# One encoder layer on one core: later weight splits, other fillers and seven ramp pairs instead of eight in the first pass over h

## The chip, the cores and the metric

The kernel runs on one core of a Trainium2 chip. The metric is the device time of one execution in microseconds (us). The engines are TensorE (PE, products and transpositions), VectorE (DVE), ScalarE (ACT), GpSimd (POOL) and SyncE (SP, which here issues most transfers). Each engine executes its instructions in the order in which they are written for it, and waits for semaphores of the others.

## The reference

One layer for x of 1024 rows and 2048 columns, all in fp32:

```python
mod = jax.nn.silu(c) @ w_ada + b_ada
shift, scale, gate = jnp.split(mod, 3, axis=-1)
h = rmsnorm(x, pre_g) * (1.0 + scale[:, None]) + shift[:, None]
proj = h @ w_in
q, k, v, gate_a, u, gate_p = jnp.split(proj, SPLIT_POINTS, axis=-1)
y_a = windowed_gqa(q, k, v, rel_table, sink) * jax.nn.silu(gate_a)
y_p = multiscale_pool(u, w_pool_grp, pool_scale) * jax.nn.silu(gate_p)
g = jax.nn.sigmoid(h @ w_merge + b_merge)
g_a, g_p = jnp.split(g, N_BRANCHES, axis=-1)
merged = g_a * (y_a @ w_br_attn) + g_p * (y_p @ w_br_pool)
o = merged @ w_out
return x + gate[:, None] * rmsnorm(o, post_g)
```

The change lies in the first third of `h @ [w_in, w_merge]`: in how h is made, and how the first columns of weights meet it.

## The kernel before, in words

**Products.** Each fp32 operand is split into a high part (ACT copies it to a format of fewer bits) and a low part (DVE subtracts); a product is then three matmuls, hi·hi, hi·lo and lo·hi. Around this stands one level of Strassen's scheme: h is held transposed in quarters, for each part j of k (four parts per pass, each of two 128-row tiles) as seven operands B11, T3, T2, B21, T4, T1, B22, each as h and l (high and low). `strassen` takes a pair of weight columns (256) and makes seven products over its parts j, into banks called X, V and Z; the sums of these (p, u) are DVE's. One pair over four parts j is 7 × 3 × 4 = 84 matmuls of 128x512, over two parts 42.

**The first pass** goes over the first half of k for 34 pairs in the order ORDER. Since h's parts become ready one by one, it has stages:

1. The start. x comes in rows (`fetch_rows_of_x`, 16 transfers for each half s of the rows). `norm_rows` squares (two pieces on ACT, two on DVE), sums (DVE) and takes the root (ACT, L428); `scale_rows` scales on DVE; PE transposes 128x128 blocks (XT); `take_turned` copies them to xT.
2. adaLN's columns. w_ada comes in groups j of 256 columns. `modulation` multiplies them by silu(c) in four steps (GEMV on PE, four k tiles in each), copies the sums (acc, ACT), transposes them (PM) and puts them into modc (DVE). In the start, `warm(n)` puts n products without use (WARM, the fillers) between the steps of group 0.
3. Plain blocks. The weights of pairs 0 to 3 come as `wide` (two transfers of 256 KB for each half, `fetch_wide`), and `wide_weights(i)` splits those of pair i into whi and wlo. `plain_blocks(i, s)` multiplies them with part j = 0 of half s of the rows, without Strassen: two banks (PB), six matmuls each, copied by ACT to c and stored to ramp_d. `fill_half(0)` makes the operands B11 and B21 for s = 0, `fill_half(1)` B12 and B22 for s = 1. Two products without use (OPEN, in the banks SEEDED) stand before the last blocks (3, 1).
4. The ramp. Pairs 4 to RAMP − 1 are done in halves: first with parts j = 0, 1 (`fill(1)` makes the operands of j = 1), their results stored to ramp_d. The side work of these pairs holds the modulation of groups 2 and 3 (`late_sums`).
5. The second stage. After `fill(2)` and `fill(3)` the pairs in SECOND (first 4 to RAMP − 1, then 0 to 3) are finished with the missing parts, and the stored ones are added by DVE (`load_parts`).
6. `pass1`: the other pairs as whole pairs, with side work (`side`) at steps listed in EASY.

All engines' orders stand as the code is written (`keep`, `pin`), the compiler's scheduler placing the rest by data. The pool of PSUM banks has two each for "mm" and "sc", in which the plain blocks alternate; a bank is free when ACT has copied it.

Of the kernel before, what the change touches and what calls it, by code (L numbers as in the profile page):

```python
# [21 lines left out]
P = 128  # L22
# [21 lines left out]
def encoder_layer(ctx: ExitStack, tc: tile.TileContext, x, c, table, w_ada, b_ada, pre_g,  # L44
# [15 lines left out]
    nc = tc.nc  # L60
# [73 lines left out]
    AHEAD_PAIRS = 4  # L134
    RAMP = 8
# [274 lines left out]
    def fetch_rows_of_x(s):  # L410
        for si in range(4 * s, 4 * s + 4):
            for q in range(4):
                xts[si, q] = slot("xt", F32)
                load(xts[si, q], x[si * P:(si + 1) * P, q * 512:(q + 1) * 512])
# [200 lines left out]
    RAMP_ORDER = [COL_K, COL_V, COL_GA, COL_GA + 256, COL_Q, COL_GA + 512, COL_GA + 768, COL_Q + 256]  # L615
# [7 lines left out]
    def ramp_raws(i, js):  # L623
        raws.append(load_raws(*weight_of(RAMP_ORDER[i]), rows_in_turn(0), js, True))

# [11 lines left out]
    fetch_rows_of_x(0)  # L637
    fetch_wide(0)
    fetch_wide(1)
    ada = [ada_slots(0)]  # L640
# [10 lines left out]
    ramp_raws(7, (0, 1))  # L651
# [59 lines left out]
    def warm(n):  # L711

        whi = weights0[0][0]
        for _ in range(n):
            keep(nc.tensor.matmul(bank("at", "WARM"), whi[:, 0, 0:P], whi.rearrange("p k n -> p (k n)"),
                                  start=True, stop=True))

    for i in range(AHEAD_PAIRS):
        wide_weights(i)
    g0 = modulation(0, ada[0].__getitem__, True, True)  # L720
    for step in g0[:3]:
        step()
        warm(5)
    ssq = norm_rows(4)
    g0[3]()
    g0[4]()
    warm(5)
    fill_half(0)
    for m in range(4):
        done = ssq  # L730
        ssq = norm_rows(5 + m) if m < 3 else None
        scale_rows(4 + m, done)
        plain_blocks(m, 0, m == 0)
# [22 lines left out]
    turn_next((6, 7))  # L756
    for tag in SEEDED:
        hi = op["B11"][0][0]
        keep(nc.tensor.matmul(bank(tag, "OPEN"), hi[:, 0:P], hi, start=True, stop=True))
    plain_blocks(3, 1)  # L760
# [19 lines left out]
    later_raws = {2: 4, 4: 5, 5: 6, 6: 7}  # L780
    for n, i in enumerate(SECOND):
        at = [(3, lambda i=SECOND[n + 1]: parts.update({i: load_parts(pev, block(ramp_d[i], 0))}))] if n < RAMP - 1 else []
        if n in later_raws:
            at.append((1, partial(second_raws, later_raws[n])))
        run(ramp_gen((1, 2, 3) if i in A else (2, 3), i, parts[i], True), side, range(7), at)
# [7 lines left out]

    ready = []
# [135 lines left out]
    EASY = ((0, 2, 4, 6), (0, 1, 3, 5, 6), (0, 2, 4, 6))  # L930
# [755 lines left out]
```

## Time and profile before

| what | us |
|---|---|
| median of 3 runs | 2106.42 |
| lowest and highest run | 2105.43, 2106.84 |
| the profiled execution | 2105.86 |
| its span | 2104.1 |
| PE busy in it | 2072.4 |
| mean granted clock of PE | 0.999 of full |

The profiled execution's time holds, beside the span of its instructions, 1.8 us around it. A busy PE may still be slower than it could be; the idle 32 us lie for the most part in the first 22 us and at the end.

### The profile page before, as it was taken

To read this page: it belongs to the slowest core of one execution; us is meant where nothing else is said; L and a number is where in the kernel's file an instruction comes from. 1 tells how busy PE (TensorE), PEld (TensorE's weight loads), DVE (VectorE), ACT (ScalarE), POOL (GpSimd) and SP (SyncE) were. 2 spreads that over 40 slices of the span, in tenths; PEclk is the share of its full clock that TensorE was granted. 3 is DMA by queue.
4 is the path that set the end of the run, shared out by engine and by line. 5 is a ranking of instruction groups with operands and counts; after the bars stand their busy time and mean duration, and the time that the engine had idled before them with its cause. 6 is when DMAs were issued, how large, how long until landed. Compare 5 with 4: busy or idle time off the path is not lost.

```text
span 2104.1 us, 28920 instructions
## 1 busy us (share of the span) xinstructions
PE 2072.4 (98%) x9475; PEld 1704.0 (81%) x9475; DVE 1550.6 (74%) x2787; ACT 1111.2 (53%) x2114; POOL 42.2 (2%) x135
## 2 busy tenths in 40 slices
PE   6999999999999999999999999999999999999998
PEld 3688788788888888888888888888888788888886
DVE  5787678787557776677777678857957977889667
ACT  5763344444574644665666444433645645767654
POOL 0100000000000000000000000010000000000000
PEclk9999999999999999999999999999999999999999
DMA  9966778998676455454545577675745556686897
GB/s 322 359 226 222 255 242 295 305 318 300 205 240 207 130 186 184 163 173 160 193 155 159 158 236 233 216 238 175 255 155 172 174 195 201 221 313 205 295 331 250
DMA packets 304171, 474.49 MB, mean 226 GB/s; under 512 B 24323, under 2 KB 144235, under 8 KB 304020
## 3 DMA queue, kind: packets, MB, share of 16 engines
q1 hardware_dynamic: 297664, 455.70, 65.6%
q0 software_dynamic: 4896, 14.73, 1.8%
q10 hardware_dynamic: 1460, 2.22, 0.3%
q8 instruction: 74, 1.21, 0.2%
q14 instruction: 77, 0.63, 0.1%
HBM read 344.60 MB, written 130.05 MB: 226 GB/s over the span
## 4 chain that ended last, share of the span: by engine, by line
PE 95%; DVE 2%; DMA 2%; ACT 0%; issue 0%; SPq 0%; DVEq 0%; ACTq 0%
PE Z L248 31%; PE V L248 21%; PE X L248 21%; PE Z L1393 2%; PE Z L1394 2%; PE Z L1395 2%; PE V L1394 1%; PE X L1394 1%; PE V L1395 1%; PE X L1395 1%; PE X L1393 1%; PE V L1393 1%; PE PT L1103 1%; PE PB L695 1%; PE GEMV L496 1%; PE PV L1114 0%
## 5 line engine op out<-in xcount | busy, mean ns | idle before, releaser
L96 ACT ACTIVATE whi<-raw 128x512 fp32r<-128x512 f32 (+2 forms) x528 | 319.2, 606 | 521.7 <-PE Z L248 263.1
L97 DVE TENSOR_TENSOR wlo<-raw,whi 128x512 fp32r<-128x512 f32 (+2 forms) x528 | 344.3, 656 | 162.7 <-PE Z L248 128.3
L97 DVE TENSOR_TENSOR wlo<-wr,whi 128x512 fp32r<-128x512 f32 x224 | 150.4, 689 | 52.2 <-ACT whi L96 49.1
L96 ACT ACTIVATE whi<-wr 128x512 fp32r<-128x512 f32 x224 | 138.0, 629 | 89.0 <-DVE wlo L97 30.0
L114 DVE TENSOR_TENSOR raw<-raw,raw 128x512 f32<-128x512 f32 (+1 forms) x80 | 54.7, 684 | 80.7 <-DMA raw<-in_w_merge_dram 59.4
L114 DVE TENSOR_TENSOR u<-V,u 128x512 f32<-128x512 f32 x94 | 64.7, 689 | 39.0 <-PE V L248 38.3
L248 PE MATMUL V<-T3h,whi 128*128 128x512 f32 x332 | 90.5, 392 | 1.3 <-ACT whi L96 1.3
L96 ACT ACTIVATE whi<-ws 128x512 fp32r<-128x512 f32 (+2 forms) x88 | 53.5, 608 | 71.5 <-PE X L248 61.9
L248 PE MATMUL Z<-B22h,whi 128*128 128x512 f32 x332 | 90.6, 392 | 0.0
L248 PE MATMUL X<-B11h,whi 128*128 128x512 f32 x332 | 90.5, 391 | 0.0
L248 PE MATMUL Z<-T1h,whi 128*128 128x512 f32 x332 | 90.4, 390 | 0.0
L248 PE MATMUL Z<-T2h,wlo 128*128 128x512 f32 x332 | 89.8, 390 | 0.6 <-DVE wlo L97 0.6
L248 PE MATMUL X<-B21h,whi 128*128 128x512 f32 x332 | 90.2, 391 | 0.0
L248 PE MATMUL V<-T4h,whi 128*128 128x512 f32 x332 | 90.1, 391 | 0.0
L248 PE MATMUL Z<-T2h,whi 128*128 128x512 f32 x332 | 90.0, 390 | 0.1
L248 PE MATMUL X<-B11l,whi 128*128 128x512 f32 x332 | 89.9, 390 | 0.0
L248 PE MATMUL Z<-B22l,whi 128*128 128x512 f32 x332 | 89.8, 390 | 0.0
L248 PE MATMUL Z<-T1l,whi 128*128 128x512 f32 x332 | 89.8, 389 | 0.0
L248 PE MATMUL V<-T3l,whi 128*128 128x512 f32 x332 | 89.8, 390 | 0.0
L248 PE MATMUL X<-B21l,whi 128*128 128x512 f32 x332 | 89.8, 390 | 0.0
L248 PE MATMUL V<-T4l,whi 128*128 128x512 f32 x332 | 89.7, 390 | 0.0
L248 PE MATMUL X<-B11h,wlo 128*128 128x512 f32 x332 | 89.7, 390 | 0.0
(370 smaller groups left out, 4881.4 us busy)
## 6 DMA issues: line engine op xcount, KB each, us to landing
part<-part_d SPq DMA_DIRECT2D x136, 256.0 KB, 4.8
ada<-in_w_ada_dram SPq DMA_DIRECT2D x128, 256.0 KB, 5.9
raw<-in_w_merge_dram SPq DMA_DIRECT2D x64, 512.0 KB, 5.7
wr<-ws_dS SPq DMA_DIRECT2D x60, 512.0 KB, 5.3
raw<-in_w_in_dram SPq DMA_DIRECT2D x56, 512.0 KB, 4.1
wr<-in_w_out_dram SPq DMA_DIRECT2D x48, 512.0 KB, 4.7
proj_d<-part SPq DMA_DIRECT2D x68, 256.0 KB, 2.3
sw<-in_w_out_dram SPq DMA_DIRECT2D x64, 256.0 KB, 5.2
```

What stands on the lines that cost most here:

```text
L96: ins = (nc.scalar.activation(hi, src, AF.Copy), nc.vector.tensor_tensor(lo, src, f32(hi), ALU.subtract))
L97: nc.vector.tensor_tensor(lo, src, f32(hi), ALU.subtract))
L114: return (eng or nc.vector).tensor_tensor(o, a, b, ALU.add)
L248: nc.tensor.matmul(ps, w_[:, i], op[mov][j][m_], start=fresh and i == 0 and n == 0, stop=i == nj - 1 and n == 2, skip_group_check=True)
L496: ins = nc.tensor.matmul(pv[g:g + 32, :], scz[:, kc, :], tile_of(kc), start=kc < 4, stop=kc >= 12, tile_position=(0, g))
L695: keep(nc.tensor.matmul(open_[nt], w[:, kh, nt * P:(nt + 1) * P], mov[kh][m], start=n == 0, stop=n == 5, skip_group_check=True))
L1103: nc.tensor.transpose(pt[:, i * P:(i + 1) * P], p[:, i * P:(i + 1) * P], ident)
L1393: nc.tensor.matmul(pb, hi, w[0], start=first, stop=False, skip_group_check=True)
L1394: nc.tensor.matmul(pb, lo, w[0], start=False, stop=False, skip_group_check=True)
L1395: nc.tensor.matmul(pb, hi, w[1], start=False, stop=last, skip_group_check=True)
```

## The change

It has six parts. (1) The transfers of w_ada group 0 are issued before those of the wide weights. (2) The fillers become `ident` times `ident` (128x128, plain fp32) into one bank instead of 128x512 products of weights in banks taken in turn, four instead of five behind each of the first three steps and behind the columns. (3) `wide_weights` stands behind the third step of group 0 for pair 0, behind `fill_half(0)` for pair 1, and between the blocks for pairs 2 and 3; before, all four stood ahead of the first step. `norm_rows(4)` moves behind `fill_half(0)`. (4) OPEN stands behind `plain_blocks(3, 1)`. (5) RAMP is 7: pair COL_Q + 256 becomes the first whole pair, and EASY has one pattern. (6) The raw weights of the first whole pair are asked for in the last pair of the ramp.

```diff
-    RAMP = 8
+    RAMP = 7
...
-    RAMP_ORDER = [COL_K, COL_V, COL_GA, COL_GA + 256, COL_Q, COL_GA + 512, COL_GA + 768, COL_Q + 256]
+    RAMP_ORDER = [COL_K, COL_V, COL_GA, COL_GA + 256, COL_Q, COL_GA + 512, COL_GA + 768]
...
     fetch_rows_of_x(0)
+    ada = [ada_slots(0)]
     fetch_wide(0)
     fetch_wide(1)
-    ada = [ada_slots(0)]
...
-    ramp_raws(7, (0, 1))
...
     def warm(n):
 
-        whi = weights0[0][0]
+        b = bank("at", "WARM")
         for _ in range(n):
-            keep(nc.tensor.matmul(bank("at", "WARM"), whi[:, 0, 0:P], whi.rearrange("p k n -> p (k n)"),
-                                  start=True, stop=True))
-
-    for i in range(AHEAD_PAIRS):
-        wide_weights(i)
+            keep(nc.tensor.matmul(b[:, 0:P], ident, ident, start=True, stop=True))
+
     g0 = modulation(0, ada[0].__getitem__, True, True)
     for step in g0[:3]:
         step()
-        warm(5)
-    ssq = norm_rows(4)
+        warm(4)
+    wide_weights(0)
     g0[3]()
     g0[4]()
-    warm(5)
+    warm(4)
     fill_half(0)
+    wide_weights(1)
+    ssq = norm_rows(4)
     for m in range(4):
+        if m < 2:
+            wide_weights(2 + m)
...
     turn_next((6, 7))
+    plain_blocks(3, 1)
     for tag in SEEDED:
         hi = op["B11"][0][0]
         keep(nc.tensor.matmul(bank(tag, "OPEN"), hi[:, 0:P], hi, start=True, stop=True))
-    plain_blocks(3, 1)
...
-    later_raws = {2: 4, 4: 5, 5: 6, 6: 7}
+    ready = []
+    later_raws = {2: 3, 3: 4, 4: 5, 5: 6}
...
+        if n == RAMP - 1:
+            at.append((3, lambda: ready.append(load_raws(*weight_of(ORDER[RAMP]), rows_in_turn(0), range(4)))))
...
-    EASY = ((0, 2, 4, 6), (0, 1, 3, 5, 6), (0, 2, 4, 6))
+    EASY = ((0, 2, 4, 6),)
```

**ACT behind fill_half(0).** These are ACT's rows between the operands of the first half (B11h, B21h) and the copies c of the first two blocks, before: two squares of norm_rows(5), the root, the copies.

```order
L551 ACTIVATE B11h_239<-xT_141,modc 128x512
L551 ACTIVATE B21h_251<-xT_143,modc 128x512
L421 ACTIVATE xt_279,ssq_630<-xt_279 128x512
L421 ACTIVATE xt_279,ssq_630<-xt_275 128x512
L428 ACTIVATE ssq_630<-ssq_630,eps_t 128x1
L700 ACTIVATE c_652<-PB_640 128x512
L700 ACTIVATE c_657<-PB_641 128x512
```

And now, from the split of pair 1 (whi_581) behind the same operands on; xt_270 is a row block of norm_rows(4), xt_278 the next:

```order
L96 ACTIVATE whi_581<-wide_232 128x256
L96 ACTIVATE whi_581<-wide_233 128x256
L421 ACTIVATE xt_270,ssq_587<-xt_270 128x512
L421 ACTIVATE xt_270,ssq_587<-xt_266 128x512
L428 ACTIVATE ssq_587<-ssq_587,eps_t 128x1
L96 ACTIVATE whi_594<-wide_232 128x256
L96 ACTIVATE whi_594<-wide_233 128x256
L421 ACTIVATE xt_278,ssq_600<-xt_278 128x512
L421 ACTIVATE xt_278,ssq_600<-xt_274 128x512
L428 ACTIVATE ssq_600<-ssq_600,eps_t 128x1
L699 ACTIVATE c_622<-PB_610 128x512
L699 ACTIVATE c_627<-PB_611 128x512
```

The squares and the root of one more row block and the splits of pairs 1 and 2 (whi from wide) have come between fill_half(0) and the copies c of the first blocks, and that of pair 3 follows them.

**ACT at fill(1).** Before, from the last split of the fourth ramp pair's weights over the copies of the last transpositions (xT) to the operands of part j = 1:

```order
L96 ACTIVATE whi_981<-raw_331 128x256
L451 ACTIVATE xT_166<-XT_223_891 128x512
L451 ACTIVATE xT_1_168<-XT_224_893 128x512
L96 ACTIVATE B11h_369<-xT_145 128x512
L96 ACTIVATE B21h_381<-xT_0_147 128x512
L96 ACTIVATE T2h_377<-tf_935 128x512
L700 ACTIVATE c_915<-PB_907 128x512
L96 ACTIVATE T1h_389<-xT_159 128x512
L96 ACTIVATE T3h_373<-xT_145 128x512
```

And now:

```order
L451 ACTIVATE xT_165<-XT_205_866 128x512
L451 ACTIVATE xT_1_167<-XT_206_868 128x512
L699 ACTIVATE c_886<-PB_878 128x512
L699 ACTIVATE c_895<-PB_879 128x512
L96 ACTIVATE whi_968<-raw_330 128x256
L96 ACTIVATE B11h_368<-xT_144 128x512
L96 ACTIVATE B21h_380<-xT_0_146 128x512
L96 ACTIVATE T2h_376<-tf_910 128x512
L96 ACTIVATE T1h_388<-xT_158 128x512
L96 ACTIVATE B22h_392<-xT_1_160 128x512
L96 ACTIVATE T3h_372<-xT_144 128x512
```

Both copies of the blocks (3, 1) now stand ahead of the first operand B11h, as does a split of weights; before, they stood behind T2h and T3h, and T3h, the sixth operand now, was the fifth.

**PE behind the third half pair.** Before, PE went from the end of the third half pair (Z with T1) into X and V of the fourth, whose operands are those of parts j = 0 and 1 (B11h_239, B11h_369), with Z with B22 of the third between:

```order
L248 MATMUL Z_1160<-T1h_259,wlo_1272 128x512
L248 MATMUL Z_1160<-T1h_389,wlo_1272 128x512
L248 MATMUL X_1285<-B11h_239,whi_1288 128x512
L248 MATMUL X_1285<-B11h_369,whi_1288 128x512
L248 MATMUL X_1285<-B11l_240,whi_1288 128x512
L248 MATMUL X_1285<-B11l_370,whi_1288 128x512
L248 MATMUL X_1285<-B11h_239,wlo_1289 128x512
L248 MATMUL X_1285<-B11h_369,wlo_1289 128x512
L248 MATMUL V_1287<-T3h_243,whi_1301 128x512
L248 MATMUL V_1287<-T3h_373,whi_1301 128x512
L248 MATMUL V_1287<-T3l_244,whi_1301 128x512
```

And now, behind the same Z with T1, the second stage's first pair stands there:

```order
L248 MATMUL Z_1135<-T1h_258,wlo_1255 128x512
L248 MATMUL Z_1135<-T1h_388,wlo_1255 128x512
L248 MATMUL X_1349<-B11h_1275,whi_1352 128x512
L248 MATMUL V_1351<-T3h_1292,whi_1365 128x512
L248 MATMUL X_1349<-B11h_1312,whi_1352 128x512
L248 MATMUL X_1349<-B11l_1276,whi_1352 128x512
L248 MATMUL Z_1135<-B22h_262,whi_1377 128x512
L248 MATMUL Z_1135<-B22h_392,whi_1377 128x512
L248 MATMUL Z_1135<-B22l_263,whi_1377 128x512
L248 MATMUL X_1349<-B11l_1313,whi_1352 128x512
L248 MATMUL X_1349<-B11h_1275,wlo_1353 128x512
L248 MATMUL X_1349<-B11h_1312,wlo_1353 128x512
```

X and V now read operands of parts j = 2 and 3 (B11h_1275 and B11h_1312, T3h_1292), which fill(2) and fill(3) make from columns of groups 2 and 3; before, such products came one half pair, 42 matmuls, later.

## Rows read from the trace of the kernel before

**Rows 1.** The page's part 1: busy us (share of span) and instructions.
```profile
PE 2072.4 (98%) x9475; PEld 1704.0 (81%) x9475; DVE 1550.6 (74%) x2787; ACT 1111.2 (53%) x2114; POOL 42.2 (2%) x135
```

**Rows 2.** Waits of PE over the run: line, releaser, us, times, longest us.
```profile
PE V L248 <- ACT whi L96: 1.3, 1, 1.3
PE PMR L884 <- DVE acc L520: 1.0, 1, 1.0
...
PE OPEN L759 <- ACT xT L451: 0.7, 1, 0.7
```

**Rows 3.** PE's timeline, 20 to 43 us: start, us, line, operation, count.
```profile
21.97 5.29 PE L443 MATMUL XT<-ident,xt 128*128 128x128 f32 x24 [1.59 <-DVE xt L434]
27.19 1.07 PE L496 MATMUL GEMV<-ada,scz 128*32 128x512 f32 x8
28.18 2.73 PE L715 MATMUL WARM<-whi 128*128 128x512 f32 x5
...
38.12 1.07 PE L496 MATMUL GEMV<-ada,scz 128*32 128x512 f32 x8
...
42.20 0.50 PE L695 MATMUL PB<-B11h,whi 128*128 128x512 f32 x1
```

**Rows 4.** SP queue's timeline, 12 to 29 us (issue of transfers).
```profile
12.58 4.66 SPq L634 DMA_DIRECT2D wide<-in_w_in_dram  x4
17.57 11.20 SPq L481 DMA_DIRECT2D ada<-in_w_ada_dram  x16
```

**Rows 5.** Transfers, 0 to 110 us: count, size, median us to landing.
```profile
wide<-in_w_in_dram SPq DMA_DIRECT2D x4, 256.0 KB, 7.4
```

**Rows 6.** DVE's timeline, 27 to 47 us.
```profile
27.97 2.77 DVE L97 TENSOR_TENSOR wlo<-wide,whi 128x256 fp32r<-128x256 f32 x8
...
44.70 0.69 DVE L423 SCALAR_TENSOR_TENSOR xt<-xt 128x512 f32<-128x512 f32 x1
...
46.31 0.15 DVE L432 RECIPROCAL rstd<-ssq 128x1 f32<-128x1 f32 x1
```

**Rows 7.** ACT's timeline, 46 to 55 us.
```profile
46.42 0.29 ACT L428 ACTIVATE ssq<-ssq,eps_t 128x1 f32<-128x1 f32 x1 [2.20 <-DVE ssq L425]
46.63 1.06 ACT L700 ACTIVATE c<-PB 128x512 f32<-128x512 f32 x2
...
52.34 2.28 ACT L700 ACTIVATE c<-PB 128x512 f32<-128x512 f32 x4
54.79 0.78 ACT L551 ACTIVATE B12h<-XT,modc 128x512 fp32r<-128x512 f32 x1 [0.17 <-PE XT L443]
```

**Rows 8.** PE's timeline, 71 to 77 us.
```profile
71.33 1.04 PE L443 MATMUL XT<-ident,xt 128*128 128x128 f32 x8
73.02 0.98 PE L759 MATMUL OPEN<-B11h 128*128 128x512 f32 x2 [0.65 <-ACT xT L451]
...
76.62 0.63 PE L248 MATMUL X<-B11h,whi 128*128 128x512 f32 x2
```

**Rows 9.** ACT's timeline, at fill(1), 73 us.
```profile
73.33 0.64 ACT L96 ACTIVATE B11h<-xT 128x512 fp32r<-128x512 f32 x1
```

**Rows 10.** PE's timeline, 112 to 123 us: fourth half pair, second stage.
```profile
112.76 0.62 PE L248 MATMUL X<-B11h,whi 128*128 128x512 f32 x2
...
122.28 0.61 PE L248 MATMUL X<-B11h,whi 128*128 128x512 f32 x2
```

**Rows 11.** DVE's timeline, 111 to 113 us.
```profile
111.48 0.55 DVE L552 TENSOR_SCALAR xT<-xT,modc 128x512 f32<-128x512 f32 x1
111.95 0.68 DVE L114 TENSOR_TENSOR u<-V,u 128x512 f32<-128x512 f32 x1
112.55 0.41 DVE L97 TENSOR_TENSOR wlo<-raw,whi 128x256 fp32r<-128x256 f32 x1
```

**Rows 12.** Windows behind PE's last product: busy us by engine, granted clock, DMA share.
```profile
2097.00:2098.00 1.00, 0.00 (x0) 0.00 (x0) 0.94 (x3) 0.29 (x1) 0.00 (x0) 1.00 0.01 2
...
2099.00:2100.00 1.00, 0.00 (x0) 0.00 (x0) 1.00 (x3) 0.00 (x0) 0.00 (x0) 0.50 0.57 209
```

More of the change, by code (lines that the diff above doesn't have):

```diff
@@ L792, in encoder_layer @@
     i = RAMP
-    ready = []
     def fetch_pair(n):
```

## The prediction

> **What bounds the kernel now.** I read the page's busy line first: TensorE (PE) is busy 98% of the span [rows 1], so only what PE waits for, or does needlessly, can be won. Next PE's waits over the whole run: about 25 us, most of them at the start (turned rows of x, the sink vector), out of reach of this change. Those the change touches are small: V for whi 1.3, PMR for acc 1.0, OPEN for xT 0.7 [rows 2]. The order of instructions is the same before and after from about 450 us on, so all is decided in the start, the ramp and the first whole pairs. Then PE's timeline of the start [rows 3]: four groups of GEMV with fillers (WARM) between them, and from 42.20 the plain blocks at one product per 0.2267 us (42 products from 112.76 to 122.28 [rows 10]). I call the start of the blocks F; it is 42.20.
>
> **Fillers and the queue: F.** A turn of GEMV and fillers took (38.12 − 27.19)/3 = 3.64 us, of which GEMV takes 0.99 (28.18 − 27.19) and five fillers 2.65 [rows 3]. No row of before has the new filler, a 128x128 plain-fp32 product. The nearest is the transposition of 128x128 fp32: eight in 1.04 us at 71.33 [rows 8], about 0.12 each from start to start, as GEMV's eight passes in 0.99. I count a plain fp32 product as two passes (a GEMV step's four products stand as x8), so four fillers are eight passes, 0.95 us. A turn becomes 1.94, three turns save 5.1, and F moves to 37.1. Bounds: with fillers at nothing the data of w_ada would set F. Its 16 transfers now go out from 12.58, where the wide ones stood, to 23.8 [rows 4]; at the 7.4 that the wide ones took to land [rows 5] the last part is there by 31.2; F follows the last GEMV by 4.08 (42.20 − 38.12), so 35.3. At 0.22 per pass, which is the transpositions' pace at 21.97 [rows 3], F is 39.5. The fillers change F alone, and whether F is worth anything is decided by the next step.
>
> **The work moved behind F.** The splits of the wide weights and norm_rows(4) stood in the shade of the fillers: wlo ran 27.97 to 30.74 while PE had fillers and GEMV [rows 6, 3]. Now only pair 0 is split ahead of the last GEMV step; the rest stands behind fill_half(0), on VectorE (DVE) and ScalarE (ACT), which must reach fill_half(1) before PE can go on with the second half of the columns. That half starts with B12h at 54.79 [rows 7], and the copies c in front of it start at 52.34, 10.14 after F. What is added to this chain:
> - the split of pair 1: two wlo of 0.345 (2.77/8 [rows 6]), 0.69;
> - norm_rows(4): squares and sum 44.70 to 46.31 in the like step [rows 6], 1.61;
> - the split of pair 2 stands between a root and the next scaling: root 0.32, ACT's half 0.40, DVE's two pieces 0.69, 1.41;
> - the split of pair 3 stands behind two copies (46.63, 1.06 for two [rows 7]): 0.32 + 1.06 + 0.40 + 0.69, less 0.98 of scaling that lies beside it and was on the chain, about 1.4.
> The idle gaps of before on the chain give back 0.27 (the 0.17 ahead of B12h among them). The sum is +4.86. So B12h comes at 37.1 + 10.14 + 4.86 + 2.28 = 54.4 against 54.79: **−0.4**, where 5.1 had been saved. What is late next is the blocks themselves. Each pair of blocks fills two banks, copied out by ACT; the third pair needs the banks of the first, and its copies now stand behind Sqrt(5), about F + 8.2 = 45.3 (before, the like root ended 46.71 having waited 2.20 for DVE [rows 7]). PE is through with two pairs of 12 products at F + 6.2 = 43.3, so it should wait about 2.5 us there, and about 1.3 and 0.9 at the next two places. These waits are no price of their own; they are where the 5.1 goes. Bounds of the term: −2.2 with F at 35.3, +2.0 with F at 39.5.
>
> **OPEN behind the last blocks.** Before, OPEN followed the last transpositions at once and waited 0.65 for xT; then came blocks (3,1) [rows 8]. Now the blocks stand first and fill that wait, but their copies, which end with the last of 12 products, stand on ACT between the two xT copies and B11h of fill(1). The blocks start at 71.33 + 0.95 = 72.28, their last product ends near 75.2, the two copies and one split follow, and B11h goes from 73.33 [rows 9] to about 76.1: 2.7 late. The sixth ACT step from there, T3h[1], follows at 0.52 each and ends about 79.4. PE starts X at 75.9 instead of 76.62 [rows 8], but waits at the first V with T3h[1], to 79.5; 11 products later its first B21 stands at 82.0, against 76.62 + 18 × 0.2267 = 80.70 before. The sum is **+1.3**, between −0.65 (the rest of the chain has slack) and +2.7 (all of the delay).
>
> **Seven ramp pairs.** A ramp pair's first half has two of four parts of k: 42 products, 9.52 us [rows 10]. The pair taken out is computed as a whole pair later, so the count of products is the same (seven matrices × 3 × 4 either way); only its four stored and reloaded parts go, which lie off PE's path. But this half was cover. While it ran, DVE and ACT did the fills of columns 2 and 3, which group 3's modulation releases (112 us). Now the second stage, whose products need these operands, begins where the half pair began, at 112.76. DVE's chain, by what stands in its order from the first modulation at 111.48 (start to start: modulation 0.47, sum 0.60, a small split 0.33, further passes 0.60 [rows 11]): to T4l it is 15 steps, two modulations, one sum 0.60, two small splits and ten passes, and ends 119.7; the first sum of a product with its stored part 0.6 more, so the first V with T4 can start at 120.5, when PE, undelayed, is there at 112.76 + 28 × 0.2267 = 119.1: 1.4. The next bank is freed at 123.2 instead of 121.4 (1.9), and Z with B22 reads its operand at 125.6 instead of 123.6 (2.0). These overlap, so the worst counts: **+2.0**. Then DVE has some 7.6 us of work for each 9.52 of PE and catches up. Bounds: 0, if the fills get ahead of the sums, and +4, two full bank waits in a row.
>
> **The first whole pairs.** PMR's 1.0 us was a wait for a DVE sum [rows 2]; with another side-step pattern it stands two products behind that sum: **−1.0** (0 to −1). V's wait for whi remains in another form, at Z: +0.1. The weights asked for a pair ahead remove no wait, since the first whole pair has none in the view of waits. The fewer stores and loads on SP's queue cost PE nothing either way. Bounds of this part together: −2.3 and +0.4.
>
> **Sum.** −0.4 + 1.3 + 2.0 − 1.0 + 0.1 = +2.0 us on the profiled execution's 2105.86, which is 2107.9. That execution was 0.56 below the median of 2106.42, so in terms of the median I say **2108.4**.
>
> **Rivals.**
> *The start passes through.* If ACT and DVE find room behind F, that is, if the moved splits and norm_rows(4) fall into their idle time (ACT's 2.20 us wait before the root [rows 7] speaks for some), the 5.1 arrives at PE, with OPEN's 0.65 and PMR's 1.0, and the second stage finds the fills done: −6.75, 2099.7. It decides from the point where B12h comes before 51. Against it: the root waited for DVE, and DVE is what gets the added work. Chance 0.13.
> *The second stage isn't absorbed (slower).* If ACT's fills, which also carry the weights' high parts, fall behind the sums, PE waits in each of the first two pairs for banks and T operands: 4 us there instead of 2.0, and 2 more if OPEN's delay is the whole 2.7 and group 3 with its fill comes later by the same. Sum about +6, 2112.4. It decides when T4 is ready over 4 us behind group 3's last modulation by more than the 28 products. For it: [rows 11] show no gap on DVE. Chance 0.12.
> *The clock.* After PE's last product, at 2096.3, the granted clock still reads 1.00 at 2097 to 2098 and 0.50, the lower of the two levels (1.2 GHz), at 2099 to 2100 [rows 12]. So a stop of PE lowers it after some time, and the stop in the blocks (2.5 us) and the two behind it are such stops. At the start the transpositions ran 5.2 us at 0.22 each before they ran at about 0.12 [rows 3, 8]; if the blocks ran so after the stop, each product would be twice as long, and some 5 us of blocks would cost up to 2.5 on PE, of which the ACT chain hides part: +0.5 to +3, about 2110.4. Against it: the stop is short, with PE busy on both sides, and nothing in the rows of before shows so short a stop lower the clock. Chance 0.10. The Trainium skill, "TensorE: Matmul & The Clock Gate", section "Part 1: The HAM clock gate", says that the throttled state is the default and that activity releases it; by that rule shorter fillers and a gap are the wrong way, and the sum would be the rival's 2110.4 instead of 2108.4. The rows of the end agree that an idle engine falls to the lower level.
> *It doesn't do what it says.* The first wide transfers are now issued behind w_ada's 16 and take 7.4 to land [rows 5], about 33.5 (two issues behind 23.8), just before the last group's column copy (34.1). ACT takes their split in order ahead of that copy; if they land 1 us later, F goes to 38.1 and the gain in the start is negative (+0.6): 2109.4. Chance 0.05.
>
> **How the numbers follow.** The forecast's own case, 0.60, spans 2105 to 2111.5 by its terms. A measurement of this kernel tells about 0.2%, 4.2 us, from no change: 2102.2 to 2110.6. The range takes in the slow rival and the better end of the start's bound, and leaves out the fast rival and tails beyond: 2102.5 to 2112.5. Of the forecast's 0.60, about 0.49 lies within 4.2 us, 0.10 above, and 0.01 below; the fast rival gives 0.13 to faster, the slow one 0.10 of its 0.12 to slower, the clock 0.07 to same and 0.03 to slower, the last all to same. Faster 0.14, same 0.63, slower 0.23.
>
> **What would show it.** Fillers: the second GEMV group some 1.9 us behind the first, the first plain block near 37. The moved work: a wait of PE for ACT's copy at the third pair of blocks, and B12h still near 54. OPEN: no wait of OPEN, a wait of V for T3h near 79. Seven pairs: waits of V and Z in the first second-stage pair, about 2 us in all. PMR's wait gone. I am wrong if B12h comes by 51, if fillers take over 0.2 us a pass, or if the second stage's first pair runs without waits.

## The result

The changed kernel takes 2114.26 us (median of 7 runs, 2111.43 to 2116.81) against 2105.26 for the kernel before (7 runs, 2104.43 to 2106.84): ratio 1.0041, 95% interval 1.003 to 1.0053. It is 9.0 us slower. The forecast was 2108.4 with a range up to 2112.5. The profiled execution of the changed kernel took 2114.77 us, 8.9 more than the one before.

The view of PE's waits in the changed kernel (line, releaser, us in total, times, longest) answers to [rows 2]. OPEN and PMR are gone from it, as forecast. New are a wait for blocks' copies (PB), two for operands of the first ramp pair (B11h, T3h), and three in whole pairs and behind them (u, whi, xt):

```profile
PE V L248 <- DVE u L114: 3.1, 2, 1.8
...
PE PB L694 <- ACT c L699: 2.4, 1, 2.4
PE b L967 <- ACT xt L978: 1.8, 1, 1.8
PE X L248 <- ACT B11h L96: 1.6, 2, 1.4
PE Z L248 <- ACT whi L96: 1.2, 1, 1.2
PE V L248 <- ACT T3h L96: 1.0, 1, 1.0
```

PE's timeline, answering to [rows 3, 8 and 10]: the last transpositions of the first half, the GEMV steps, the first block, the third pair of blocks, the first block of the second half, the first ramp pair and the first sum of the second stage:

```profile
20.54 5.15 PE L443 MATMUL XT<-ident,xt 128*128 128x128 f32 x24 [1.54 <-DVE xt L434]
25.61 1.07 PE L496 MATMUL GEMV<-ada,scz 128*32 128x512 f32 x8
26.61 1.16 PE L714 MATMUL WARM<-ident 128*128 128x128 f32 x8
27.70 1.06 PE L496 MATMUL GEMV<-ada,scz 128*32 128x512 f32 x8
...
35.97 0.50 PE L694 MATMUL PB<-B11h,whi 128*128 128x512 f32 x1 [0.70 <-ACT B11h L551]
...
44.73 0.50 PE L694 MATMUL PB<-B11h,whi 128*128 128x512 f32 x1 [2.41 <-ACT c L699]
...
53.72 0.50 PE L694 MATMUL PB<-B12h,whi 128*128 128x512 f32 x1 [0.34 <-ACT B12h L551]
...
75.59 0.50 PE L248 MATMUL X<-B11h,whi 128*128 128x512 f32 x1 [1.41 <-ACT B11h L96]
...
78.32 0.47 PE L248 MATMUL V<-T3h,whi 128*128 128x512 f32 x1 [0.98 <-ACT T3h L96]
...
80.93 0.61 PE L248 MATMUL X<-B21h,whi 128*128 128x512 f32 x2
...
113.79 0.50 PE L248 MATMUL X<-B11h,whi 128*128 128x512 f32 x1 [0.21 <-ACT B11h L96]
...
120.85 0.73 PE L248 MATMUL V<-T4h,whi 128*128 128x512 f32 x2 [0.32 <-DVE p L114]
...
123.68 0.70 PE L248 MATMUL X<-B11h,whi 128*128 128x512 f32 x2 [0.26 <-DVE part L114]
```

A trap stands in the first row. The 24 transpositions begin at 20.54, in the execution before at 21.97 [rows 3]; over the 20 traces of this study they begin between 20.20 and 22.36, as x lands, though the transfers of x's first half stand first in all. So all starts are compared from that row on:

| us behind the 24 transpositions' start | before | changed | forecast of the difference |
|---|---|---|---|
| first block (F) | 20.23 | 15.43 | −5.1 |
| B12h's first product | 33.65 | 33.18 | −0.4 |
| first B21 of the ramp | 58.75 | 60.39 | +0.9 |
| last product | 2073.91 | 2084.10 | +2.0 |

F and B12h came as forecast to 0.3 us. (The B21 of before is the row X<-B21h,whi at 80.72, the last product stands at 2095.88.) Of the 10.2 us by which the last product is later, 1.6 arise ahead of that B21; the execution's time shows 8.9, since x landed 1.4 sooner.

The rest is read from the starts of X with B11h, which begins each pair (19.04 us for a whole pair without a wait). From that B21 to the second of the 26 whole pairs that both kernels still have then it takes 157.1 us in place of 154.5, the second stage's price of 2.6. This pair and the next take 43.4 in place of 39.7 (+3.7): in the changed kernel 20.5, with the wait of 1.21 for whi at Z, and 22.8, with the wait of 1.84 for u and products at half rate behind it; in the kernel before 19.0 and 20.6.

```profile
263.34 1.48 PE L248 MATMUL V<-T3h,whi 128*128 128x512 f32 x4 [1.84 <-DVE u L114]
```

The two pairs around PMR take 39.8 together where they took 42.0 (−2.2); the stretch from there to the attention's first transposition (PT) 489.8 against 486.6 (+3.2, of it 1.23 and 1.80 the waits of V at 535.76 and of b at 607.34); and PT to the end +1.3. That is 1.6 + 2.6 + 3.7 − 2.2 + 3.2 + 1.3 = 10.2.

### The profile page after: what moved, and what is told of

The parts are those of the page before. It is cut to its first block, busy times and chain, and to the rows that moved or that the text cites. A ratio compares the mean times of both kernels' runs of the same rounds, so it can differ in the third digit from the quotient of the medians.

```text
span 2113.0 us, 28876 instructions
## 1 busy us (share of the span) xinstructions
PE 2073.2 (98%) x9489; PEld 1704.6 (81%) x9489; DVE 1543.0 (73%) x2770; ACT 1106.2 (52%) x2104; POOL 42.2 (2%) x135
## 3 DMA queue, kind: packets, MB, share of 16 engines
q8 instruction: 74, 1.21, 0.3%
## 4 chain that ended last, share of the span: by engine, by line
PE 89%; DMA 4%; issue 3%; DVE 3%; ACT 1%; POOL 0%; SPq 0%; DVEq 0%; POOLq 0%; ACTq 0%
PE Z L248 31%; PE V L248 21%; PE X L248 20%; PE Z L1394 2%; PE Z L1396 2%; PE Z L1395 2%; DMA ada<-in_w_ada_dram 1%; PE V L1396 1%; PE V L1394 1%; PE V L1395 1%; PE X L1396 1%; PE X L1395 1%; PE X L1394 1%; DMA xt<-in_x_dram 1%; PE PT L1104 1%
## 5 line engine op out<-in xcount | busy, mean ns | idle before, releaser
L248 PE MATMUL V<-T3h,wlo 128*128 128x512 f32 x332 | 90.1, 391 | 0.0
L248 PE MATMUL Z<-T2l,whi 128*128 128x512 f32 x332 | 89.8, 389 | 0.0
```

What stands on the lines that cost most here:

```text
L248: nc.tensor.matmul(ps, w_[:, i], op[mov][j][m_], start=fresh and i == 0 and n == 0, stop=i == nj - 1 and n == 2, skip_group_check=True)
```

## The experiments

Times are medians; each series has its own runs of the kernel before beside it. "B21" is the first B21 of the ramp behind the 24 transpositions' start, as in the table.

### The change in two halves, once more, and bias_d in eight pieces

e1 is the changed kernel again, for a trace.

> The changed kernel once more, for one trace. Theory A (waits that the change makes): the first two waits in whole pairs stand again at the same products, Z with B22 for ACT's whi about 1.2 us near 245 and V with T3 for DVE's u about 1.8 us near 263, and so do the three late ones (V near 536, 1.2; b near 607, 1.8; V near 2045, 0.8). Theory B (the late three are transfers that happened to land late): the first two stand again, at least two of the late three are gone or stand at other products, and the time may differ by 1 to 3 us from 2114.8.

One run, 2115.43. The first two waits came back at the same products (1.20 at 245.26, 1.72 at 263.64, this time without the lower clock: that pair took 21.1 instead of 22.8), and so did the late ones, at 533.54 (0.35), 605.19 (1.91) and 2045.29 (0.84); a wait of 1.03 for u at 1236.05 is new. So all five stand at the same products, as Theory A has it, and their sizes vary from one execution to the next: they are weak places of this kernel.

e2 is the kernel before with parts 5 and 6 (RAMP 7, its lists, one pattern, the early request); e3 the changed kernel with these undone.

```diff
-    RAMP = 8
+    RAMP = 7
...
-    EASY = ((0, 2, 4, 6), (0, 1, 3, 5, 6), (0, 2, 4, 6))
+    EASY = ((0, 2, 4, 6),)
```

> The kernel before with parts 5 and 6 alone (seven ramp pairs, one pattern, weights a pair ahead), the start left as it was. Theory A: second stage +2.5, the stall behind the 2 MB transfer bias_d +3.7, PMR -2.2, so +4 alone and up to +8 with the late waits: 2109 to 2113. Theory C (the start is to blame, by its stops of PE and the lower clock behind them): within 1 us of before, 2105 to 2106.5.

> The changed kernel with parts 5 and 6 undone (eight ramp pairs, three patterns, no early request): parts 1 to 4 alone. Theory A: 0 to +1 us, 2105 to 2106.5, since the start reaches the first ramp pair's B21 0.2 us later than before. Theory C: most of the 9 us, 2111 or more.

e2: 2110.37 (11 runs, 2109.09 to 2111.39) against 2106.16, ratio 1.0019 (1.001 to 1.0028): +4.2. Its trace has the second stage's +2.6, the waits of Z (1.20) and V (1.79, pair of 22.8) and the PMR pairs' −2.2. e3: 2108.33, ratio 1.0012 (1.0003 to 1.0021): +2.2, B21 at 60.91. So both halves cost, seven pairs more; theory C falls as the whole cause, and Theory A's 0 to +1 for the start was too low. Together they make 6.4 of 9.0; the three intervals, about 2 us either way each, do not tell the rest of 2.6 from nothing.

e4 writes bias_d in eight transfers:

```diff
-        keep(nc.scalar.dma_start(bias_d.rearrange("h (p l) -> h p l", l=LINE),
-                                 bass.AP(line_d.tensor, line_d.offset, [[LINE, NH], [0, P], [1, LINE]])))
+        keep(nc.scalar.dma_start(bias_d[h:h + 1].rearrange("h (p l) -> h p l", l=LINE),
+                                 bass.AP(line_d.tensor, line_d[h].offset, [[LINE, 1], [0, P], [1, LINE]])))
...
+    then.update({6 - AHEAD + 2 * h: partial(bias_lines, h) for h in range(NH)})
```

> The changed kernel with bias_d written by eight transfers of 256 KB, two side steps apart, instead of one of 2 MB. Theory A (the one transfer holds the queue's others back): the waits of Z near 245 and V near 263 are gone, and with them the lower clock at 263 to 268: -3 to -4 us against the changed kernel, 2110 to 2111.5. Rival (the two waits come from the side step's place in the pair, whatever transfer stands there): the waits stay, 2114.

2115.6 (5 runs), ratio 1.0046 (1.0032 to 1.0059): no gain. The wait of V is gone, but that of Z stands in four pairs, each of 20.6 us (in the second and fourth PMR's products fill most of the gap):

```profile
245.25 1.21 PE L248 MATMUL Z<-B22h,whi 128*128 128x512 f32 x4 [1.21 <-ACT whi L96]
...
265.83 1.21 PE L248 MATMUL Z<-B22h,whi 128*128 128x512 f32 x4 [0.23 <-ACT whi L96]
...
286.41 1.21 PE L248 MATMUL Z<-B22h,whi 128*128 128x512 f32 x4 [1.21 <-ACT whi L96]
...
306.99 1.21 PE L248 MATMUL Z<-B22h,whi 128*128 128x512 f32 x4 [0.23 <-ACT whi L96]
```

So there are two prices. The 2 MB transfer makes V's wait; the issue itself, while ACT has it, makes Z's, 1.5 us for each such pair. ACT's rows in the changed kernel show why: behind the issue stand three reads of products (u, Z, p) in one piece, and the weight splits that usually alternate with them come after, so Z, which PE could have started at 243.67, waits for its weights.

```profile
232.84 0.75 ACTq L870 DMA_DIRECT2D bias_d<-line_d  x1
238.27 0.60 ACT L305 ACTIVATE u<-Z 128x512 f32<-128x512 f32 x1 [4.84 <-PE Z L248]
241.05 0.58 ACT L288 ACTIVATE Z<-X 128x512 f32<-128x512 f32 x1 [2.18 <-PE X L248]
...
244.21 2.18 ACT L96 ACTIVATE whi<-raw 128x512 fp32r<-128x512 f32 x4
```

The kernel before pays that once too, at V (1.3 of [rows 2]; its pair takes 20.6), behind an issue that stands at another place of its pair:

```profile
246.33 0.75 ACTq L869 DMA_DIRECT2D bias_d<-line_d  x1
```

How the 2 MB make V wait is in SP's view of waits (200 to 300 us) and SP's timeline of the changed kernel: a load of w_ada stands in SP's queue until bias_d has ended, and the next pair's raw weights stand behind it.

```profile
SPq L532 <- DMA bias_d<-line_d: 10.4, 1, 10.4
```

```profile
240.01 12.23 SPq L532 DMA_DIRECT2D ada<-in_w_ada_dram  x4
252.34 0.41 SPq L198 DMA_DIRECT2D raw<-in_w_in_dram  x1
...
254.39 0.51 SPq L198 DMA_DIRECT2D raw<-in_w_in_dram  x1
```

The raw weights' two halves are asked for at 252.34 and 254.39, and DVE gets the second at 261.99; behind its use of that half (ws) stands u, which reads V's bank. V could have started at 261.5 and started at 263.34. In the kernel before the same load waited 4.5 us.

```profile
261.99 0.69 DVE L117 TENSOR_TENSOR ws<-raw 128x512 f32<-128x512 f32 x1 [1.44 <-DMA raw<-in_w_in_dram]
262.60 0.68 DVE L114 TENSOR_TENSOR u<-V,u 128x512 f32<-128x512 f32 x1
```

### Moving bias_d, OPEN and the pattern of side steps

```diff
-        keep(nc.scalar.dma_start(bias_d.rearrange("h (p l) -> h p l", l=LINE),
+        keep(nc.gpsimd.dma_start(bias_d.rearrange("h (p l) -> h p l", l=LINE),
```

> The changed kernel with bias_d's one 2 MB transfer issued by POOL in place of ACT; the orders of ACT, DVE and SP are then those of pairs without it. Theory A2 (the price lies in ACT's order around the issue, 1.5 us, and in SP's queue, where a load of w_ada waits for bias_d's end with the next pair's raw weights behind it, 2.0 to 3.7 us): the waits of Z near 245 and V near 263 are gone, 2109 to 2111 against the changed kernel's 2114.3. Rival (the 2 MB themselves take the bandwidth, whoever issues them): Z's wait gone, V's stays, 2112 to 2113.

e5: 2113.27 (5 runs), ratio 1.0034 (1.0021 to 1.0046). Z's wait is gone, V waits 0.69 and 0.66 in two pairs of 20.2 and 20.0: the two prices, 5.3 in the changed kernel's trace, are 2.1 here. POOL waits for no side step and issues at 209.4, and the raw weights of the first whole pairs are then late: a half asked for at 210.93 reached DVE at 223.05, while the 2 MB were under way. Both theories hold in part.

e6 puts OPEN back ahead of the blocks (3, 1).

```diff
+    for tag in SEEDED:
+        hi = op["B11"][0][0]
+        keep(nc.tensor.matmul(bank(tag, "OPEN"), hi[:, 0:P], hi, start=True, stop=True))
     plain_blocks(3, 1)
```

> The changed kernel with OPEN ahead of the blocks (3, 1) as before. Theory A: the first ramp pair's B21 comes 2.1 us sooner behind the last 24 transpositions (58.3 in place of 60.4), with OPEN's wait of 0.65 back: 2112 to 2112.5. Rival (the two copies are late whatever stands first, since the chain of ACT is late since the blocks): B21 stays near 60.4, 2114.

2115.09 (5 runs), ratio 1.004 (1.0027 to 1.0052), and B21 at 61.53, later by 1.1 and not sooner by 2.1. OPEN's place is not the cause. ACT still has the copies ahead of B11h in this kernel.

e7 is the changed kernel with EASY's three old patterns, e8 the kernel before with bias_d on POOL and steps at 0, 2, 4, 6.

```diff
-    EASY = ((0, 2, 4, 6), (0, 1, 3, 5, 6), (0, 2, 4, 6))
+    EASY = ((0, 2, 4, 6),) * 16 + ((0, 2, 3, 4, 6),)
```

> The changed kernel with the three old patterns of side steps. Theory A: the PMR wait is back (+2.2), and bias_d is issued one product earlier in its pair, so the load of raw weights behind it comes some 3 to 5 us sooner and V's wait near 263 is gone (-2 to -3.7): 2112.5 to 2114.5. If the wait near 263 hangs on seven pairs alone, it stays: 2116.

> The kernel before with bias_d issued by POOL and with side steps at 0, 2, 4, 6 in each pair (the last of the 17 has a fifth, since one step would be left over); nothing else of the change. Theory A2: V's wait near 258 goes (-1.5) and PMR's (-2.2): 2102 to 2103. Rival: what PE gains there is given back in late transfers behind 500 us: 2105 to 2106.

e7: 2112.48 (7 runs, 2108.4 to 2115.22), ratio 1.0026 (1.0015 to 1.0037); in its trace PMR's pair is long again (21.9) and V's wait near 263 is gone (19.2). So that wait hangs on the pattern: it sets in which product bias_d is issued. e8: 2108.38 (11 runs, 2103.23 to 2110.52), ratio 1.0007 (0.9998 to 1.0016), although its trace, the shortest of its runs, has neither V's nor PMR's wait: the rival was right, the gain is given back in most executions.

### One part alone, and a better place for bias_d

e9 has the new fillers (`warm` with ident, four of them) and nothing else.

```diff
-            keep(nc.tensor.matmul(bank("at", "WARM"), whi[:, 0, 0:P], whi.rearrange("p k n -> p (k n)"),
-                                  start=True, stop=True))
+            keep(nc.tensor.matmul(b[:, 0:P], ident, ident, start=True, stop=True))
```

> The kernel before with the new fillers alone (four of 128x128 in one bank); loads, splits, norm_rows(4) and all else in their old places. Theory D (the chain of row blocks on DVE and ACT sets the second half of the blocks, and the moved splits and norm_rows(4) ate what the fillers gave): the first block starts some 2 to 3 us sooner behind the last 24 transpositions (17.5 to 18, it was 20.2; the loads of w_ada now bound it), and B12h 1 to 2.5 us sooner than 33.65: 2104 to 2105.3 against 2106.2. Rival (the chain is bound by the landing of x's second half): B12h stays at 33.65, 2106.

2106.39 (11 runs), ratio 1.0001 (0.9993 to 1.001). F at 20.88 and B12h at 34.60 did not come sooner. PE's and ACT's timelines:

```profile
32.76 2.65 PE L496 MATMUL GEMV<-ada,scz 128*32 128x512 f32 x8
39.54 0.66 PE L464 MATMUL PM<-ident,acc 128*128 128x128 f32 x4 [4.14 <-ACT acc L503]
```

```profile
36.33 0.63 ACT L421 ACTIVATE xt<-xt 128x512 f32<-128x512 f32 x1 [9.44 <-DMA xt<-in_x_dram]
...
38.91 0.58 ACT L503 ACTIVATE acc<-GEMV 128x512 f32<-128x512 f32 x1
```

The fourth GEMV step ends at 35.4, but the copy of its sums stands on ACT behind norm_rows(4), which waits for the second half of x until 36.33. By these rows, and not by a run of its own, moving norm_rows(4) is what frees F; what the earlier transfers of w_ada add was not taken apart. The chain of row blocks then decides B12h.

e10 writes the copies of blocks (3, 1) behind fill(1) in the changed kernel.

```diff
     fill(1)
+    for f in late_puts:
+        f()
```

> The changed kernel with the two copies of blocks (3, 1), and with them their stores on POOL, written behind fill(1): on ACT B11h to T3h then stand ahead of the copies, on POOL the 14 memsets that open the operands' slots ahead of the two stores. Theory A3 (the 2.1 us between B12h and the first B21 are these two orders): PE's waits for B11h and T3h go, B21 comes at 58.3 to 58.8 behind the last 24 transpositions in place of 60.4, and the time is about 2 us below the changed kernel's, 2112 to 2112.7. Rival: another wait takes their place, 2114.

2113.95 (5 runs), ratio 1.0037 (1.0024 to 1.0049), B21 at 60.28: the rival. B11h came 1.1 sooner, and V waited 1.38 for its bank, which a copy has to free.

e11 is the kernel before with bias_d on POOL alone; e12 adds parts 1 to 4 and the late copies to it.

> The kernel before with bias_d issued by POOL and nothing else. Theory E (the pattern 0, 2, 4, 6 of side steps makes late transfers, which ate the gain of the last such kernel): V's wait near 258 gone and no late waits: 2104.5 to 2105, that is 1.5 below before. Rival (the transfer of bias_d at another time harms by itself): 2106 to 2108.4, as with the pattern.

> Parts 1 to 4 of the change with eight ramp pairs and the three old patterns, the two late copies behind fill(1), and bias_d issued by POOL. If A3 and E hold: start -0.5, OPEN's wait -0.65, bias_d -1.5, so 2103 to 2104.5, below both kernels. If the start's other waits stay: 2105 to 2107.

e11: 2103.83 (11 runs, 2101.73 to 2107.3) against 2106.34, ratio 0.999 (0.9981 to 0.9999): the only kernel here with an interval below the kernel before, though it ends at 0.9999. Its third whole pair takes 19.0 where it took 20.6. e12: 2106.34, ratio 0.9998 (0.9989 to 1.0007), B21 at 61.98: the start takes back what bias_d gives.

### What stands between B12h and B21

e13 is the changed kernel with e6's and e10's edits together, e15 the kernel before with OPEN moved and nothing else, e16 the start without OPEN's move (eight pairs, old patterns, late copies, bias_d on POOL); e14 is the changed kernel with the old patterns and bias_d on POOL.

```diff
+    plain_blocks(3, 1)
     for tag in SEEDED:
         hi = op["B11"][0][0]
         keep(nc.tensor.matmul(bank(tag, "OPEN"), hi[:, 0:P], hi, start=True, stop=True))
-    plain_blocks(3, 1)
```

> The changed kernel with OPEN ahead of the blocks (3, 1) as before and the two copies of these blocks behind fill(1). Theory A4 (PE's order and ACT's order at this place cost 2 us only together: with OPEN last, V waits for a bank that a copy has to free; with the copies first, X and V wait for their operands): B21 at 58.3 to 58.8 behind the last 24 transpositions, 2111.5 to 2112.5. Rival (POOL's or DVE's queue is late since the blocks, whatever the order): B21 stays over 60, 2114.

> The changed kernel with the three old patterns of side steps and bias_d issued by POOL. Theory F (the pattern makes the late waits; the rest of the price is start +2.2 and second stage +2.6): 2106.3 + 2.2 + 2.6 - 2.0 (bias_d) = 2109 to 2110, no wait of V near 263 or 536. Rival (late transfers come with seven pairs in any case): 2112 or more.

> The kernel before with OPEN behind the blocks (3, 1), part 4 alone. The forecast's own third term: B21 1.3 us later (60.05 in place of 58.75 behind the last 24 transpositions), bounds -0.65 and +2.7. Theory A4: V waits for the bank that the second copy frees, +0.5 to +1.5, 2106.8 to 2107.8. Rival (no price without the moved start): -0.65, 2105.7.

> Parts 1 to 3 of the change with eight pairs and the old patterns, OPEN as before, the copies of blocks (3, 1) behind fill(1), bias_d issued by POOL. Theory A4: B21 at 58.3 (-0.5), so -0.4 against the kernel before with bias_d on POOL (2103.8): 2103 to 2104. Rival: a wait stays in the start, 2105 to 2106.

e15: 2106.2 (11 runs), ratio 1.0001 (0.9992 to 1.0009), B21 at 58.68: OPEN's move alone costs nothing and gains nothing. e13: 2119.63 (6 runs), ratio 1.006 (1.0048 to 1.0072), B21 at 62.89; e16: 2108.49 (11 runs), ratio 1.0011 (1.0003 to 1.002), B21 at 62.18 though B12h came at 32.30. Theory A4 falls. e14: 2115.29 (5 runs, 2108.94 to 2115.74), ratio 1.0043 (1.003 to 1.0056); its profiled execution took 2108.94, as Theory F has it, the others 5 to 7 more.

ACT's timeline of e16 shows what holds the operands back, from the copies of the last turned columns (xT) on:

```profile
70.53 1.08 ACT L451 ACTIVATE xT<-XT 128x512 f32<-128x512 f32 x2
74.97 0.42 ACT L96 ACTIVATE whi<-raw 128x256 fp32r<-128x256 f32 x1 [3.37 <-PE PB L697]
75.30 0.61 ACT L96 ACTIVATE B11h<-xT 128x512 fp32r<-128x512 f32 x1
```

A weight split waits 3.37 us for PE's last blocks, with all operands of fill(1) behind it. It is the fourth split of the first ramp pair, for the product with B21. Four buffers hold split weights; the four plain pairs fill them, so this split can only start when the blocks of pair 3 have been computed. Before, it stood behind fill(1), the first of the two splits in this row (whi_981, shown with the change, is the third split of that pair):

```profile
79.00 0.71 ACT L96 ACTIVATE whi<-raw 128x256 fp32r<-128x256 f32 x2
```

With the moved start the scheduler puts it (whi_968 in the order shown with the change) ahead of B11h. e17 holds back this one split in e16:

```diff
+        with behind(hold and "fill1", "v"), behind(hold and "fill1", "a"):
+            w = prep(a12)
-        product(prep(a12), "B21", bx)
+        product(w, "B21", bx)
```

> The kernel of e16 with one more change: the fourth weight split of the first ramp pair (whi and wlo, for the product with B21) is written to stand behind fill(1) on ACT and DVE. Theory A5 (four buffers hold the split weights; the four plain pairs fill them, and this split waits on ACT for the end of the last blocks, with all of fill(1) behind it): B11h comes right behind the copies of xT, PE's waits for B11h and T3h go, B21 at 58.5 to 59.5 in place of 62.2 behind the last 24 transpositions, the time 2.5 to 3.5 us below e16's, 2105 to 2106. Rival: V's wait for the bank keeps B21 over 61, 2108.

2105.81 (11 runs) against 2106.98, ratio 0.9996 (0.9987 to 1.0006), B21 at 58.83 in place of 62.18. Theory A5 holds: this split is the price of the start in e16. What is left of the start still gains nothing, since e11, with the old start, has B21 at 58.46 and 2103.83. In e17 PE waits for neither B11h nor T3h:

```profile
PE PB L700 <- ACT c L705: 3.4, 2, 2.4
...
PE OPEN L768 <- ACT xT L454: 0.7, 1, 0.7
```

e18 is e14 once more, for its trace.

> The kernel of e14 once more, for its trace. Theory B (transfers that land late, by chance, at places with no slack): with a time near 2115, waits for a transfer's data at places where e14's trace has none, 4 to 6 us of them with the lower clock behind them; with a time near 2109, none.

It took 2113.43, 4.5 more than e14's profiled run. Its waits are e14's, each a little longer (1.08 and 1.54 near 233 and 244 against 0.85 and 1.09; one more of 0.99 at the blocks), with only small ones added; the rest is spread over the run, 2.4 us of it behind the attention. So no single late transfer explains it, and Theory B is not shown in the form given.

## Why the prediction was wrong

Between the profiled executions the forecast missed 6.9 us: some 0.7 in the start, 0.6 in the second stage, 2.4 in the first whole pairs and 4.5 behind them, less 1.4 for x's landing.

**Fillers, right.** F came 4.8 sooner (5.1 forecast). A turn took 27.70 − 25.61 = 2.09 (1.94 forecast); four fillers stand as x8 with 1.09 from start to start.

**The work behind F, right.** B12h came 0.5 sooner (0.4), and PE waited 2.41 at the third pair of blocks (2.5). The 1.3 and 0.9 forecast at the next two places are not in this trace. By e9, the fillers without the move are worth nothing either: ACT's order then holds the sums.

**The clock: the rival's mechanism, without price at this place.** The forecast gave it 0.10 and argued that so short a stop does not lower the clock. Behind that stop the granted clock fell. Windows of the changed kernel (columns as in [rows 12], granted clock third from the end):

```profile
44.00:45.00 1.00, 0.27 (x1) 0.27 (x2) 0.85 (x2) 1.00 (x3) 0.02 (x1) 1.00 1.10 357
45.00:46.00 1.00, 1.00 (x5) 0.77 (x5) 0.50 (x2) 1.00 (x4) 1.00 (x2) 0.83 1.10 348
46.00:48.00 2.00, 2.00 (x7) 1.54 (x6) 1.83 (x8) 1.21 (x5) 0.09 (x1) 0.50 1.11 349
48.00:49.00 1.00, 1.00 (x4) 0.81 (x3) 1.00 (x3) 1.00 (x3) 0.03 (x1) 0.50 1.06 384
49.00:50.00 1.00, 1.00 (x6) 0.84 (x5) 0.97 (x3) 0.97 (x4) 1.00 (x2) 0.97 1.08 407
```

0.50 is the lower level, 1.2 GHz; eight products ran at up to 0.43 each instead of 0.2267, which cost PE about 1.6 us. This fall agrees with the Trainium skill, "TensorE: Matmul & The Clock Gate", section "Part 1: The HAM clock gate": idleness brings the throttled state back. But it does not come each time: all 14 traces with the moved start have this stop, of 2.39 to 2.43 us; in ten of them the clock reads 0.50 behind it, in four (e5, e12, e17, e18) 1.00, and there PE waits 0.99 at the next place. B12h comes at 32.30 to 33.70 in the ten and at 33.70 to 33.84 in the four, so it did not suffer: DVE and ACT set it. The same fall behind the late u (263 to 267) did cost: the pair there took 22.8, in e1's trace without the fall 21.1.

**OPEN, +1.3 forecast, 2.1 measured, and the wrong culprit.** The forecast saw that two copies and one split stand ahead of B11h on ACT, and put that down to OPEN's move. e15 shows OPEN's move to cost nothing, e17 that the split, placed there by the scheduler because of the moved start, costs 3.35 (62.18 − 58.83) in e16. I had counted this split as work and not asked which buffer it writes. That it is also what costs the changed kernel its 2.1 is argued from these runs: no run holds it back there. In e10 and e13, which have seven pairs and the copies behind fill(1), it waits 1.73 and 3.36 for PE's last blocks; in the changed kernel the copies ahead of it do this waiting. Part of the wait in the changed kernel was POOL's besides: the memset that opens B11h's slot now stands behind both stores of these blocks' copies.

```profile
74.22 0.54 POOL L700 DMA_DIRECT2D ramp_d<-c  x1 [0.85 <-ACT whi L96]
74.75 0.12 POOL L565 MEMSET B11h<- 128x1 f32 x1
```

```profile
73.83 0.41 ACT L96 ACTIVATE whi<-raw 128x256 fp32r<-128x256 f32 x1
74.90 0.63 ACT L96 ACTIVATE B11h<-xT 128x512 fp32r<-128x512 f32 x1 [0.67 <-POOL B11l L565]
```

**Seven pairs, +2.0 forecast, 2.6 measured.** V with T4h starts at 120.85 (120.5 forecast), but PE comes there late itself and waits 0.32 for it, not 1.4; with the waits for B11h and for the sum with a stored part that makes 0.8 us, and no wait of Z stands there. The rest are the restarts and changes between X, V and Z that the new order brings, which I had not counted.

**The whole pairs, −0.9 forecast, +1.5 measured, and the first step that failed.** The forecast said: "V's wait for whi remains in another form, at Z: +0.1", and: "The fewer stores and loads on SP's queue cost PE nothing either way." The first was right (1.21 at Z). The second failed, and the new pattern was priced by PMR alone: with it bias_d was issued 13.8 us into its pair instead of 11.1, ended later in the next one, and held the raw weights in SP's queue, which made the pair behind 3.8 longer (2.0 in e1); with the old patterns, in e7, that wait is gone. I had read PE's waits, and not which instruction of SP's queue waits for what, and what stands behind it. PMR's gain was 2.2 and not 1.0, since the wait's restart and its neighbours went as well.

**What was put at nothing, the second step that failed and the largest.** The forecast said: "The order of instructions is the same before and after from about 450 us on, so all is decided in the start, the ramp and the first whole pairs." The late waits (V near 536, b near 607) and the longer end make +4.5 in the profiled pair of kernels. Nor is PE's order quite the same there: near 530 us GATE's eight products stand between X and V's first products (T3h) in the eight traces with seven pairs and the new pattern, and elsewhere in the other twelve; V's wait near 536 stands in five of these eight and in none of the twelve. From PMR's pairs to the last product the eleven traces with seven pairs take 1702.7 to 1709.3 us (mean 1706.5), the nine with eight pairs 1702.3 to 1705.8 (mean 1704.0); the kernel before's 1702.8 lies near the low end. So 2.6 of the 4.5 is a difference of the means, and the rest lies within what traces differ by.

b's rows of x are asked for 3.4 to 5.1 us into their pair in the 20 traces, and ACT has them 9.8 to 11.9 us into it (9.94 in the kernel before, 11.80 in the changed one); PE waits for all beyond 10.0, with eight pairs too (0.9 in e15).

In the stretch from the last PT to the last product, where all kernels execute the same instructions, the nine traces with eight pairs take 898.0 to 900.4 us (mean 899.3) and the eleven with seven pairs 898.7 to 903.6 (mean 901.3); the ranges overlap, and e14 and e18, one kernel, lie 2.4 apart. About half of the difference stands in PE's waits there, in these traces all for split weights: 3.0 in e13's (903.6), 2.3 in e5's (902.5), 0.6 in the kernel's before (898.5), none in e9's (898.0). This is not what e2 and e3 leave of the 9.0, since e2 has seven pairs and its time holds it. That rest answers to the stretch ahead: from PMR's pairs to the first PT the changed kernel's two traces take 489.8 and 490.6, e2's 486.6, e3's 487.0, and the kernel before's 486.6.

Why the rows of x come later, and why seven pairs, which only leave one stored block of 1 MB less in DRAM by then, go with a slower stretch that comes 700 us later, is open: where the tensors lie in DRAM was not tried.

## What to carry to other kernels

A step that is moved in a kernel whose order a scheduler makes moves others with it: for each instruction that lands ahead of a critical one, ask which buffer it writes and who still reads that buffer, since in an in-order engine its wait becomes everybody's. Where a queue serves both a big slow transfer's waiters and the next weights, look at what stands behind the waiter; issuing one 2 MB transfer from an idle engine gave about 2.5 us here (0.2 to 4.0 by its interval), while the six parts of the change cost 9.0. And compare two traces from an event that both reach, not from zero: here the landing of x alone shifted them by up to 2.2 us.

## What the runs showed of the hardware that was not expected

An issue of a transfer on ACT takes 0.48 us in e4's trace (0.75 for the 2 MB in one), but it cost PE 1.5 us in each of e4's four pairs, through the order made around it. A stop of PE of 2.4 us at the same place lowered the granted clock in ten of 14 traces and not in the other four. A load on SP's queue waited 10.4 us for a transfer that another engine had issued. And the same instructions took between 898.0 and 903.6 us over the last stretch, from one kernel's trace to another's, with a granted clock of 1.00 in each 50 us of it in e13's and e5's (the last few us apart).
